# Inputs laid out by features, split without normalization, and 1/rms multiplied in after the products

## The chip, the cores and the metric

The kernel runs on one core of a Trainium2 chip. The metric is device time in microseconds (us) of one execution, as the median of several runs. The core has a matrix engine (TensorE; PE in the profile, PEld for its weight loads), three engines for elementwise work (VectorE is DVE, ScalarE is ACT, GpSimd is POOL), and SyncE (SP), which issues the DMAs in this kernel. Products land in PSUM, eight banks of 128 partitions x 512 float32.

## What is computed

Two transformer blocks, one after the other, on x of 256 tokens x 1024 features, in float32. Only the beginning of the first and the two memories matter here:

```python
h = rms_norm(x, g_pre_mix)                     # x / rms(x) * gain, over the 1024 features
q, k, v, z, xbc, dt_raw, ga, gs = split(h @ w_in)
o_att = stick_breaking_attention(q, k, v)      # 16 heads
o_ssm = ssm_branch(z, conv(xbc), dt_raw, ...)  # 32 heads, causal convolution of 4 taps, chunks of 128
merged = sigmoid(ga) * (o_att @ w_br_att) + sigmoid(gs) * (o_ssm @ w_br_ssm)
x = x + rms_norm(merged @ w_mix_out, g_post_mix)
x = x + rms_norm(memory_cross_attention(rms_norm(x, g_pre_xa), rms_norm(mem, g_mem), ...), g_post_xa)
x = x + rms_norm(swiglu(rms_norm(x, g_pre_ffn), ...), g_post_ffn)
# second block: two layers of attention (the first with a forget gate, "fox", the second with latent
# projections, "mla"), each also attending to rmsnorm(mem_2, mem_norm_2), and a convolved FFN
```

## The kernel before

The 256 tokens are two tiles of 128. Weights come from HBM in units of 128 x 1024 words (512 KB), and each is split into a high and a low float32r part, whose sum is the float32 value; activations are split in the same way. A product of two split values is three matmuls (high x high, high x low, low x high) that add up in one PSUM bank. The split of a unit is a copy to the high part (ACT, sometimes DVE) and a subtraction for the low part (DVE, sometimes POOL). Ten split units are held (NB) and four raw ones (RAW); SP's queue loads the next unit when a raw place is free.

All work is written as Python generators ("threads": main(0), main(1) for the tiles, mix_both, sb, ssd, memory, prepare for the weights and so on). Program.run() lets the thread go on that could start first by a rough model of the engines' times (class Model), with priorities, and so writes down the order of the instructions on each engine; that order is fixed in the program. A thread can wait for an event ("w"), a buffer of the arena ("b", "m"; 17,600 words for each partition in all), a bank ("p"), a split unit ("u") or a time ("r", "f"). A product is emitted only when its banks and its unit are there.

For a product the contraction must lie on the partitions, so the activations are needed transposed. prenorm_joint() (line 733) does this for x (g_pre_mix), mem (g_mem) and mem_2 (mem_norm_2): rms() squares the tile on ACT and sums it, rsqrt() adds and takes the power on POOL, two copies multiply the tile by 1/rms, transpose_split() (687) transposes its eight blocks on TensorE, and split_half() (701) multiplies by the gain and splits, block by block. The tiles' splits lie side by side in a Joint.

At the start build() (1960) loads x's first tile, the gains, two weight units, x's second tile and more units; first_consts() (1990) has TensorE run 22 transposes of the identity (WARM). main(t) (908) then makes its split and two products for v, which main(1) can make only after main(0) has begun the same unit. mix_both() (988) makes the products of both tiles at once that are wanted with the features on the partitions, by proj_joint() (768; two banks each): q and k (qk_both, 1025), dt (dt_both, 1085), B and C, and four groups of x and z. The convolved ones go through taps() (1038), which reads the bank for one ACT operation and three DVE operations for each of its two blocks; z goes through Silu (z_both, 1078). sb() does the stick-breaking attention in four lanes, ssd_quad() (1242) the state space model. In ssd_quad a row of acsT is spread over all partitions by a matmul with a column of pick (1254), both on 64 partitions, followed by matmuls that add a mask. memory() (1474) runs beside the rest: mem when the third of the four groups of the state space model is done, mem_2 after the first FFN's up products.

Nearly all elementwise operations are recorded at line 290, DMAs at 547, matmuls at 539 and transposes at 543, so in the profile they are told apart by tile names and shapes: wr is a raw unit, wh and wl its split, arena_r the split activations, pa PSUM, arena nearly everything else.

## Time and profile before

| | us |
|---|---|
| time, median of 3 runs (1333.91 to 1334.86) | 1334.74 |
| span of the profiled execution, from its first to its last instruction | 1330.6 |
| TensorE busy | 1289.8 |
| VectorE busy | 909.7 |
| ScalarE busy | 816.8 |
| GpSimd busy | 285.1 |

The times of the runs are of other executions than the profiled one, whose own time the profile gives only as its span. The profile's parts are: busy time by engine, the same in slices over the span, DMA queues, the chain of work that ended last, groups of instructions with mean duration and the idle time ahead of them, and the DMA issues. Matmuls are pipelined, so the duration of one is longer than the distance from its start to the next one's; where TensorE's pace is wanted, the distance between starts is read. A timeline row with "x2" holds two instructions that follow each other.

### The profile page before, as it was taken

What the parts mean: (1) busy time and instruction counts of PE and PEld (TensorE: products, weight loads), DVE (VectorE), ACT (ScalarE), POOL (GpSimd) and SP (SyncE); (2) the same over time, 40 slices, a digit from 0 to 9 for tenths busy, and PEclk for the clock granted to TensorE, in tenths of its full rate; (3) what the DMA queues carried; (4) which work ended last, traced back from release to release, by engine and by line L of the source; (5) the groups of instructions that cost most, each with busy time, mean ns of one, the idle gap of its engine ahead of it and who ended that gap; (6) DMA issues with size and microseconds to landing.
All of it is one profiled execution on the core that took longest, in us unless ns stands there. A gap on an engine that the chain in (4) does not pass through costs nothing.

```text
span 1330.6 us, 22067 instructions
## 1 busy us (share of the span) xinstructions
PE 1289.8 (97%) x8376; PEld 1146.3 (86%) x8376; DVE 909.7 (68%) x1471; ACT 816.8 (61%) x1481; POOL 285.1 (21%) x364
## 2 busy tenths in 40 slices
PE   8999999999999999999998899998999989999998
PEld 6989998898888887999997788788999867799997
DVE  6567688877677537655556567898665897786664
ACT  6567677766646547544456566785554785865552
POOL 3052203333022002000014521102111463031110
PEclk9999999999999999999999999998999999999999
DMA  8632543544664624756552343566654333365650
GB/s 270 219 112 96 195 154 107 180 158 143 216 211 159 227 73 143 246 183 188 190 192 96 127 143 112 191 221 221 190 185 144 115 112 99 131 223 189 185 173 32
DMA packets 62457, 217.95 MB, mean 164 GB/s; under 512 B 7440, under 2 KB 7568, under 8 KB 62352
## 3 DMA queue, kind: packets, MB, share of 16 engines
q1 hardware_dynamic: 62352, 216.56, 49.9%
q8 instruction: 65, 1.06, 0.3%
q14 instruction: 40, 0.33, 0.1%
HBM read 215.48 MB, written 1.05 MB: 163 GB/s over the span
## 4 chain that ended last, share of the span: by engine, by line
PE 79%; DVE 9%; POOL 5%; ACT 3%; issue 2%; DMA 2%; SPq 0%; DVEq 0%; POOLq 0%; ACTq 0%
PE pa L539 75%; DVE arena L290 6%; POOL arena L290 4%; PE pa L543 3%; DVE wl L290 2%; ACT arena L290 2%; POOL small L290 1%; ACT wh L290 1%; DVE arena_r L290 1%; DMA wr<-in_w_in 1%; ACT arena_r L290 0%; DMA arena<-in_mem 0%; DMA wr<-in_w_up 0%; DMA wr<-in_w_dn 0%; SPq L547 0%
## 5 line engine op out<-in xcount | busy, mean ns | idle before, releaser
L539 PE MATMUL pa<-wh,arena_r 128*128 128x512 f32 (+2 forms) x1812 | 590.8, 395 | 3.6 <-DVE arena_r L290 1.6
L290 DVE TENSOR_TENSOR wl<-wr,wh 128x1024 fp32r<-128x1024 f32 (+2 forms) x353 | 432.4, 1233 | 219.9 <-ACT wh L290 214.4
L290 ACT ACTIVATE wh<-wr 128x1024 fp32r<-128x1024 f32 (+3 forms) x393 | 406.2, 1044 | 246.5 <-PE pa L539 200.2
L539 PE MATMUL pa<-arena_r,wh 128*128 128x256 f32 (+2 forms) x2736 | 495.5, 283 | 0.0
L539 PEld LDWEIGHTS pa<-arena_r,wh 128*128 128x128 f32 (+2 forms) x2736 | 425.6, 190 | 4.3 <-issue 0.3
L539 PEld LDWEIGHTS pa<-wh,arena_r 128*128 128x128 f32 x1812 | 342.3, 190 | 73.2 <-DVE arena_r L290 3.3
L539 PE MATMUL pa<-arena_r,wl 128*128 128x256 f32 (+2 forms) x1368 | 385.5, 282 | 0.0
L539 PE MATMUL pa<-wl,arena_r 128*128 128x512 f32 (+2 forms) x906 | 353.2, 390 | 4.2 <-DVE wl L290 4.1
L539 PEld LDWEIGHTS pa<-arena_r,wl 128*128 128x128 f32 (+2 forms) x1368 | 259.9, 190 | 0.2
L290 POOL TENSOR_TENSOR wl<-wr,wh 128x1024 fp32r<-128x1024 f32 (+2 forms) x53 | 131.0, 2476 | 568.0 <-ACT wh L290 543.7
L539 PEld LDWEIGHTS pa<-wl,arena_r 128*128 128x128 f32 x906 | 172.0, 190 | 35.4 <-DVE wl L290 5.4
L290 ACT ACTIVATE arena<-pa 128x512 f32<-128x512 f32 (+4 forms) x142 | 78.5, 563 | 73.8 <-PE pa L539 58.9
L290 DVE SCALAR_TENSOR_TENSOR arena<-pa,cols,arena 128x255 f32<-128x255 f32 (+2 forms) x208 | 89.1, 476 | 31.2 <-ACT arena L290 29.6
L290 DVE TENSOR_TENSOR arena<-arena 128x512 f32<-128x512 f32 (+4 forms) x117 | 90.8, 792 | 23.1 <-POOL arena L290 13.3
L290 ACT ACTIVATE arena<-arena 128x512 f32<-128x512 f32 (+5 forms) x126 | 76.6, 615 | 33.7 <-DVE arena L290 30.6
L539 PE MATMUL pa<-arena 128*64 128x128 f32 (+4 forms) x888 | 91.2, 286 | 3.2 <-POOL arena L290 1.7
L539 PEld LDWEIGHTS pa<-arena 128*64 128x64 f32 (+3 forms) x888 | 78.1, 160 | 16.4 <-issue 5.5
L543 PE MATMUL pa<-ident,arena 128*128 128x128 f32 (+3 forms) x494 | 73.1, 278 | 18.1 <-DVE arena L290 14.0
L543 PEld LDWEIGHTS pa<-ident,arena 128*128 128x128 f32 (+3 forms) x494 | 56.8, 138 | 33.9 <-DVE arena L290 19.1
L290 POOL TENSOR_SCALAR small<-small 128x1 f32<-128x1 f32 x38 | 17.4, 459 | 265.6 <-ACT arena L290 186.9
L290 ACT ACTIVATE arena<-pa,cols 128x256 f32<-128x256 f32 x92 | 44.8, 566 | 28.2 <-PE pa L539 28.2
L290 ACT ACTIVATE arena<-pa,small 128x128 f32<-128x128 f32 (+4 forms) x126 | 44.5, 416 | 21.9 <-PE pa L539 21.6
(123 smaller groups left out, 769.8 us busy)
## 6 DMA issues: line engine op xcount, KB each, us to landing
wr<-in_w_up SPq DMA_DIRECT2D x96, 512.0 KB, 4.0
wr<-in_w_in SPq DMA_DIRECT2D x80, 512.0 KB, 4.3
wr<-in_w_gu SPq DMA_DIRECT2D x44, 512.0 KB, 4.1
wr<-in_w_dn SPq DMA_DIRECT2D x44, 512.0 KB, 4.2
wr<-in_w_down SPq DMA_DIRECT2D x22, 512.0 KB, 4.0
wr<-in_w_fox SPq DMA_DIRECT2D x20, 512.0 KB, 3.3
wr<-in_w_br_ssm SPq DMA_DIRECT2D x16, 512.0 KB, 4.2
wr<-in_w_xkv SPq DMA_DIRECT2D x16, 512.0 KB, 4.1
```

Of the source, the lines that this page charges most:

```text
L290: emit = (lambda: f(*a, **k)) if f else (lambda: None)
L539: self.T.matmul(out, l, r, start=start, stop=stop, skip_group_check=True)
L543: self.T.transpose(out, in_, self.const["ident"][:k, :k])
```

## The change

The host also lays out x, mem and mem_2 by features (x_T, mem_T and mem_2_T: 128 partitions, 8 blocks of features, 256 tokens). split_T() makes the split of (input * gain) from these, without transposes and without 1/rms, for both tiles at once. inv_rms() finds 1/rms of the tokens from the input as it was laid out before, which is loaded as well. Products with the tokens on the partitions are multiplied by 1/rms in the copy out of PSUM (a value for each partition); those with the features on the partitions by a [128, 256] tile R that has 1/rms of the tokens along each row, in a DVE multiplication (scaled()). spread() makes R: the identity times 1/rms, then a product with ones. For q and k the multiplication takes the place of the copy; for z, and ahead of the convolutions, it is an operation of its own, whose result goes to SBUF, from where Silu and the taps go on. Beside this, pick and acsT are used on all 128 partitions, with zeros in the upper 64, ones is set earlier, and the first loads come in another order. Comments and docstrings are left out of the file, so its lines have other numbers. The diff without these, cut to its core:

```diff
+    def load_T(self, name, half):
+        s = slice(1024 * half, 1024 * half + 1024)
+        self.dma(self.st["T", name].ap[:, s], self.d[name + "_T"][:, s])
+
+    def split_T(self, name, gain, X):
+        src = self.st["T", name].ap.rearrange("p (k t c) -> p k t c", k=8, t=2)
+        H, L = X.both
+        for k in range(8):
+            g = self.c(C_GAIN + 8 * GAINS.index(gain) + k)
+            yield self.act(H[:, k], src[:, k], "Copy", scale=g)
+            yield self.V.scalar_tensor_tensor(L[:, k], src[:, k], g, H[:, k].bitcast(F32), op0=OP.mult, op1=OP.subtract)
+            self.set((("T", name), k))
+
+    def inv_rms(self, name, t, x=None, r=None):
+        x = x or (yield from self.load_x(name, t))
+        r = self.st["r", name, t] = self.col() if r is None else r
+        yield from self.rms(x.ap, r)
+        x.free()
+        self.set(("r", name, t))
+
+    def spread(self, name):
+        w = yield ("b", 256)
+        for t in range(2):
+            yield ("w", ("r", name, t))
+            yield self.V.tensor_scalar(w.ap[:, 128 * t:128 * t + 128], self.const["ident"], self.st["r", name, t], None,
+                                       op0=OP.mult)
...
+        self.mm(b[1][:, :256], self.const["ones"], w.ap, True, True, 0.43)
+        yield self.copy(w.ap, b[1][:, :256])
...
     def main(self, t):
-        yield ("w", "ident")
-        x = st["x0", t]
         J = ("X", "g_pre_mix")
-        X = yield from self.prenorm_joint(t, x.ap, "g_pre_mix")
-        self.set(("first", "second")[t])
-        x.free()
+        X = st[J].tile(t)
         st["v", t] = yield ("b", D)
         for i in range(2):
-            b = yield from self.proj(X, self.cb("w_in", 4 + i), 2, 512)
-            yield self.copy(st["v", t].ap[:, 512 * i:512 * i + 512], b[1])
+            b = yield from self.proj(X, self.cb("w_in", 4 + i), 2, 512, parts=("T", "x"))
+            yield ("w", ("r", "x", t))
+            yield self.copy(st["v", t].ap[:, 512 * i:512 * i + 512], b[1], scale=st["r", "x", t])
...
-            yield self.act(sg.ap[:, s], b[1], "Sigmoid")
+            yield self.act(sg.ap[:, s], b[1], "Sigmoid", scale=st["r", "x", t])
...
+    def first_split(self):
+        st = self.st
+        yield from self.split_T("x", "g_pre_mix", st["X", "g_pre_mix"])
+        self.set("second")
+        st["T", "x"].free()
+        self.st["R"] = yield from self.spread("x")
+        self.set("R")
+
+    def scaled(self, dst, b, rows=slice(0, 128), scale=None):
+        d, p = (a.rearrange("p (f n) -> p f n", f=2)[rows] for a in (dst, b[1]))
+        if scale is None:
+            return self.V.tensor_tensor(d, p, self.by_rows()[rows], op=OP.mult)
+        return self.V.scalar_tensor_tensor(d, p, scale, self.by_rows()[rows], op0=OP.mult, op1=OP.mult)
...
     def mix_both(self, J):
-        yield ("w", (J, 1))
+        yield ("w", (("T", "x"), 7))
...
     def qk_both(self, bs, q, c):
+        yield ("w", "R")
             if q:
-                yield self.copy(st["qT"].ap[:, s], bs[i][1], scale=0.125)
+                yield self.scaled(st["qT"].ap[:, s], bs[i], scale=0.125)
             else:
                 for k in range(2):
-                    r = slice(64 * k, 64 * k + 64)
-                    yield self.copy(st["kT%d" % k].ap[r, s], bs[i][1][r])
+                    yield self.scaled(st["kT%d" % k].ap[:, s], bs[i], slice(64 * k, 64 * k + 64))
...
-    def taps(self, b, u, base, n):
+    def taps(self, b, u, base, n, norm=False):
         yield ("f", b[1])
+        x = None
+        if norm:
+            yield ("m", [512], [])
+            x = yield ("b", 512)
+            yield self.scaled(x.ap, b)
+            self.fbank(b)
+        u, p = (a.rearrange("p (j c) -> p j c", j=2) for a in (u, x.ap if norm else b[1]))
...
     def z_both(self, bs, g):
         for i in range(2):
-            yield self.act(z.ap[:, 512 * i:512 * i + 512], bs[i][1], "Silu")
+            yield self.scaled(z.ap[:, 512 * i:512 * i + 512], bs[i])
             self.fbank(bs[i])
+        yield self.act(z.ap, z.ap, "Silu")
...
     def ssd_quad(self, g, q, ys):
-                self.mm(b[1][:, 256 * j:256 * j + 256], const["pick"][:64, h:h + 1].to_broadcast([64, 128]),
-                        const["acsT"][:64, :], j == 0, False, 0.109)
+                self.mm(b[1][:, 256 * j:256 * j + 256], const["pick"][:, h:h + 1].to_broadcast([128, 128]),
+                        const["acsT"], j == 0, False, 0.109)
...
     def memory_norm(self, name, gain):
-        evs = [self.spawn(self.memory_tile(t, name, gain), self.cur.prio, 1) for t in range(2)]
+        st = self.st
+        st["T", name] = yield ("b", 2 * D)
+        for h in range(2):
+            self.load_T(name, h)
+        evs = [self.spawn(self.inv_rms(name, t), self.cur.prio, 1) for t in range(2)]
+        yield ("m", [], [2 * D, 2 * D])
+        X = st["X", gain] = Joint(self.memr)
+        yield from self.split_T(name, gain, X)
+        st["T", name].free()
         for e in evs:
             yield ("w", e)
...
     def memory(self):
         X = yield from self.memory_norm("mem", "g_mem")
+        R = yield from self.spread("mem")
             for i in range(2):
-                yield self.copy(st["kTx"].ap[:, 1024 * c + 512 * i:1024 * c + 512 * i + 512], bs[i][1])
+                k = st["kTx"].ap[:, 1024 * c + 512 * i:1024 * c + 512 * i + 512]
+                yield self.V.tensor_tensor(k.rearrange("p (f n) -> p f n", f=2), bs[i][1].rearrange("p (f n) -> p f n", f=2),
+                                           R.ap[:, None, :].to_broadcast([128, 2, 256]), op=OP.mult)
...
     def build(self):
-        for t in range(2):
-            self.st["x0", t] = self.buf(D)
-        list(self.load_x("x", 0, self.st["x0", 0]))
+        self.st["T", "x"] = self.buf(2 * D)
+        x = [self.buf(D) for _ in range(2)]
         g = slice(C_GAIN, C_CONV)
+        self.load_T("x", 0)
         self.dma(self.const["cols"][:, g], self.d["cols"][:, g])
         if not self.plan:
             self.load(2)
-        list(self.load_x("x", 1, self.st["x0", 1]))
+        self.load_T("x", 1)
+        if not self.plan:
+            self.load(RAW)
+        for t in range(2):
+            list(self.load_x("x", t, x[t]))
```

## Rows read from the trace of the kernel before

**Rows 1.** The page, part 1: busy time of each engine, its share of the span, instructions.
```profile
PE 1289.8 (97%) x8376; PEld 1146.3 (86%) x8376; DVE 909.7 (68%) x1471; ACT 816.8 (61%) x1481; POOL 285.1 (21%) x364
```
**Rows 2.** Windows by stage, from several questions: stretch in us, its length, busy time of PE, PEld, DVE, ACT and POOL (instructions), then TensorE's granted clock as a share of full, the busy share of the DMA engines, GB/s.
```profile
0.00:22.00 22.00, 16.22 (x71) 13.04 (x72) 13.14 (x18) 14.60 (x29) 7.88 (x14) 0.92 0.78 264
...
12.10:15.30 3.20, 3.17 (x8) 2.50 (x9) 3.13 (x9) 3.20 (x8) 0.00 (x0) 0.51 0.86 300
...
22.00:300.00 278.00, 275.01 (x2075) 251.62 (x2074) 199.11 (x311) 191.55 (x351) 80.70 (x108) 1.00 0.48 157
300.00:1331.00 1031.00, 998.57 (x6232) 881.64 (x6231) 697.49 (x1143) 610.66 (x1103) 196.50 (x245) 0.99 0.50 163
...
1000.00:1200.00 200.00, 190.32 (x1221) 164.96 (x1220) 161.95 (x323) 136.35 (x296) 64.97 (x75) 1.00 0.44 139
...
220.00:240.00 20.00, 19.48 (x183) 18.45 (x182) 18.07 (x29) 13.46 (x21) 6.11 (x3) 1.00 0.65 218
```
**Rows 3.** Waits of TensorE over the whole span, the largest: us in total, times, longest.
```profile
PE pa L543 <- DVE arena L290: 14.0, 10, 2.6
```
**Rows 4.** Timeline of TensorE at the start: start, us, instruction, in brackets the idle time before and what ended it.
```profile
9.09 0.47 PE L539 MATMUL pa<-wh,arena_r 128*128 128x512 f32 x1 [1.01 <-DVE wh L290]
10.26 0.50 PE L539 MATMUL pa<-wl,arena_r 128*128 128x512 f32 x1 [0.70 <-DVE wl L290]
12.13 1.22 PE L539 MATMUL pa<-wh,arena_r 128*128 128x512 f32 x2 [1.36 <-DVE arena_r L290]
...
16.20 0.39 PE L539 MATMUL pa<-wl,arena_r 128*128 128x512 f32 x1
16.42 0.62 PE L539 MATMUL pa<-wh,arena_r 128*128 128x512 f32 x2
16.88 0.39 PE L539 MATMUL pa<-wl,arena_r 128*128 128x512 f32 x1
```
**Rows 5.** Windows, of the matmuls of line 539 alone: stretch, its length, busy time of PE and PEld (instructions), granted clock, DMA share, GB/s.
```profile
0.00:21.40 21.40, 9.57 (x31) 6.73 (x31) 0.92 0.79 268
```
**Rows 6.** The chain that ended last in 0 to 80 us, in order of time: start, us, what.
```profile
21.40 41.76 PE pa L539 x290
```
**Rows 7.** Timeline of all engines at the start: the split of the first units, and 1/rms of x's second tile.
```profile
8.25 0.69 DVE L290 CAST wh<-wr 128x1024 fp32r<-128x1024 f32 x1 [1.32 <-DMA wr<-in_w_in]
8.98 1.23 DVE L290 TENSOR_TENSOR wl<-wr,wh 128x1024 fp32r<-128x1024 f32 x1
...
9.50 1.06 ACT L290 ACTIVATE wh<-wr 128x1024 fp32r<-128x1024 f32 x1 [1.45 <-DMA wr<-in_w_in]
...
14.72 0.66 ACT L290 ACTIVATE arena<-arena 128x512 f32<-128x512 f32 x1
...
16.56 1.55 POOL L290 TENSOR_TENSOR small<-small,mhalf 128x1 f32<-128x1 f32 x1
```
**Rows 8.** Groups of instructions of one shape over the whole span: busy us, mean ns of one, then the idle time before them and what ended it.
```profile
L539 PE MATMUL pa<-arena_r,wh 128*128 128x256 f32 x2688 | 489.0, 284 | 0.0
...
L290 DVE TENSOR_TENSOR arena_r<-arena,arena_r 128x256 fp32r<-128x256 f32 x66 | 29.9, 484 | 6.5 <-ACT arena_r L290 6.5
...
L290 DVE TENSOR_TENSOR arena<-pa,arena 128x512 f32<-128x512 f32 x37 | 25.3, 687 | 12.5 <-PE pa L539 11.4 <-ACT arena L290 1.1
L290 ACT ACTIVATE arena_r<-arena 128x256 fp32r<-128x256 f32 x66 | 24.6, 409 | 28.1 <-DVE arena L290 27.1 <-PE pa L539 1.0
...
L539 PE MATMUL pa<-arena 128*128 128x256 f32 x64 | 15.3, 384 | 0.5 <-DVE arena L290 0.5
...
L539 PE MATMUL pa<-acsT,pick 64*128 64x256 f32 x32 | 8.0, 329 | 0.0
```
**Rows 9.** Timelines where the memories are transposed (mem at 309.76, mem_2 at 696.54 us).
```profile
309.76 0.66 PE L543 MATMUL pa<-ident,arena 128*128 128x128 f32 x4 [1.75 <-ACT arena L290]
...
696.54 1.91 PE L543 MATMUL pa<-ident,arena 128*128 128x128 f32 x16
```
**Rows 10.** Timelines of TensorE in a product for both tiles (50 us) and in the state space model (198 us).
```profile
50.00 0.40 PE L539 MATMUL pa<-arena_r,wh 128*128 128x256 f32 x2
...
50.36 0.40 PE L539 MATMUL pa<-arena_r,wh 128*128 128x256 f32 x2
...
198.35 0.28 PE L539 MATMUL pa<-arena_r,wl 128*128 128x256 f32 x1
198.56 0.50 PE L539 MATMUL pa<-acsT,pick 64*128 64x256 f32 x2
198.99 0.28 PE L539 MATMUL pa<-negmaskT,identb 128*128 128x256 bf16 x1
199.20 0.50 PE L539 MATMUL pa<-acsT,pick 64*128 64x256 f32 x2
199.64 0.28 PE L539 MATMUL pa<-negmaskT,identb 128*128 128x256 bf16 x1
```
**Rows 11.** Timeline around 698 us: a weight split on POOL and an addition on DVE.
```profile
697.88 2.39 POOL L290 TENSOR_TENSOR wl<-wr,wh 128x1024 fp32r<-128x1024 f32 x1 [0.37 <-ACT wh L290]
698.33 2.49 DVE L290 TENSOR_TENSOR arena<-arena 128x512 f32<-128x512 f32 x1
```
**Rows 12.** Timeline of one group of heads of the stick-breaking attention: its first operation out of PSUM and a split of its output.
```profile
63.19 0.69 DVE L290 TENSOR_SCALAR arena<-pa 128x512 f32<-128x512 f32 x1 [0.82 <-PE pa L539]
...
77.41 0.38 ACT L290 ACTIVATE arena_r<-pa 128x256 fp32r<-128x256 f32 x1 [0.62 <-PE pa L539]
```

More of the change, by code (lines that the diff above doesn't have):

```diff
@@ L603, in row_done, with proj @@
             e[0].free()
-    def proj(self, X, keys, kper, width, k0=0):
+    def proj(self, X, keys, kper, width, k0=0, parts=None):
         yield ("p", 1)
@@ L731, in prenorm @@
         return X, r, ev
+    def load_T(self, name, half):
[21 more added lines that the diff above has]
+                                       op0=OP.mult)
+        yield ("w", "ones")
+        yield ("r", w.ap, self.const["ones"])
+        yield ("p", 1)
+        b = self.bank()
+        self.mm(b[1][:, :256], self.const["ones"], w.ap, True, True, 0.43)
+        yield self.copy(w.ap, b[1][:, :256])
+        self.fbank(b)
+        return w
     def prenorm_joint(self, t, src, name):
@@ L1048, in taps @@
                                             op0=OP.mult, op1=OP.add)
-        self.fbank(b)
+        if norm:
+            x.free()
+        else:
+            self.fbank(b)
     def conv_both(self, bs, i0, dst, ev):
-        evs = [self.spawn(self.taps(bs[i], dst.ap[:, 512 * i:512 * i + 512], C_CONV + 20 * i0 + 10 * i, 4))
+        evs = [self.spawn(self.taps(bs[i], dst.ap[:, 512 * i:512 * i + 512], C_CONV + 20 * i0 + 10 * i, 4, True))
                for i in range(2)]
@@ L1460, in gated_both @@
             self.set(("h", "w_gu", c, t))
-    def memory_tile(self, t, name, gain):
-        x = yield from self.load_x(name, t)
-        yield from self.prenorm_joint(t, x.ap, gain)
-        x.free()
     def memory_norm(self, name, gain):
-        evs = [self.spawn(self.memory_tile(t, name, gain), self.cur.prio, 1) for t in range(2)]
+        st = self.st
[7 more added lines that the diff above has]
+        st["T", name].free()
         for e in evs:
             yield ("w", e)
-        return self.st["X", gain]
+        for t in range(2):
+            self.set((("X", gain), t))
+        return X
     def memory(self):
@@ L1489, in memory @@
             for n in range(2):
-                yield self.copy(st["vx", n].ap[:, 512 * c:512 * c + 512], bs[n][1])
+                yield self.copy(st["vx", n].ap[:, 512 * c:512 * c + 512], bs[n][1], scale=st["r", "mem", n])
                 self.fbank(bs[n])
@@ L1917, in constants2 @@
         yield from tri(c["negmaskT"], 1, OP.is_ge, 0.0, -1e30)
-        yield G.memset(c["ones"], 1.0)
+        yield G.memset(c["acsT"][64:].bitcast(F32), 0.0)
+        yield G.memset(c["pick"][64:].bitcast(F32), 0.0)
         yield V.tensor_copy(c["identb"], c["ident"])
@@ L1970, in build @@
             self.load(2)
-        list(self.load_x("x", 1, self.st["x0", 1]))
+        self.load_T("x", 1)
+        if not self.plan:
+            self.load(RAW)
+        for t in range(2):
+            list(self.load_x("x", t, x[t]))
+        self.st["X", "g_pre_mix"] = Joint(self.memr)
         self.st["halo"] = self.buf(96)
@@ L1976, in build @@
         self.spawn(self.first_consts(), 0)
+        self.spawn(self.first_split(), 0, -0.5)
+        for t in range(2):
+            self.spawn(self.inv_rms("x", t, x[t]), 0, 0.5)
+        self.set("begun")
         if not self.plan:
-            self.load(RAW)
             self.spawn(self.prepare(), 0, lambda: self.urgency(self.unit_at))
@@ L1993, in first_consts @@
         self.set("ident")
+        yield self.G.memset(c["ones"], 1.0)
+        self.set("ones")
         b = self.bank()
@@ L2091, in layout @@
     d["x"], d["mem"], d["mem_2"] = a["x"][0], a["mem"][0], a["mem_2"][0]
+    for k in ("x", "mem", "mem_2"):
+        d[k + "_T"] = np.ascontiguousarray(d[k].T.reshape(8, 128, S).transpose(1, 0, 2)).reshape(128, 8 * S)
     pick = lambda n: a[n[:-2]][int(n[-1])] if n[-2] == "." else a[n].reshape(1024)
```

22 lines of the change are left out of this document (16 added, 6 removed).

## The prediction

> **What bounds the kernel now.** I read the page's busy times first: TensorE is busy for 97% of the span, VectorE (DVE) for 68%, ScalarE (ACT) for 61% [rows 1]. So time can go only where TensorE gets less to do, or where it stands still. The windows by stage tell where it stands: in 0 to 22 us it is busy for 16.2 of 22, in 22 to 300 us (the mixer, most of what the change touches) for 275.0 of 278, and after 300 us it stands 32.4 of 1031 us [rows 2]. The waits of TensorE say on whom: 14.0 us on DVE ahead of transposes, and everything else is smaller [rows 3]. Nothing in the mixer stands long, so a gain there must be instructions that TensorE no longer runs or runs faster, and a loss must be a new wait. At the start the reader should look at the gaps in the list of matmuls [rows 4]: the weight products begin at 9.09 us, stop for the low half of the weights and then for 1.36 us for the split of x, and get dense only after 13 us. In 12.10 to 15.30 us the granted clock was 0.51 of full [rows 2], so the lower level of 1.2 GHz, after a stretch in which the engine mostly stood.
>
> All terms are set against the profiled span, 1330.6 us. The median of the runs is 4.1 us above it (1334.74); I take that distance as unchanged.
>
> **Part 1, the start.** Up to 21.4 us TensorE has run 31 weight products [rows 5]. In the dense stretch a low-half product starts at 16.20 and the next at 16.88 us, with two high-half ones between [rows 4]: 0.68 / 3 = 0.227 us each. 31 x 0.227 = 7.0 us of useful work, so 21.4 - 7.0 = 14.4 us go to the warm-up, the 16 transposes of x and waiting. From 21.4 us on the chain shows TensorE alone for 41.8 us [rows 6], so a microsecond saved earlier arrives there whole.
> After the change the first product needs the first unit's weights and k blocks 0 to 3 of x_T. The weights come last: their high half is cast at 8.25 us, when the transfer has landed, and their low half is ready at 8.98 + 1.23 = 10.2 us [rows 7]; as many bytes lie ahead of them as before, with one DMA issue fewer. A block of x_T costs an ACT copy of 128x256 (0.41 us) and a DVE subtraction (0.48 us, a two-input DVE operation of that size) [rows 8], so four blocks take about 2 us of either engine and are done by 8 us. From then on both tiles can use each unit: 12 x 0.227 = 2.7 us of products for a unit whose split costs 1.06 us on ACT and 1.23 us on DVE [rows 7], so no wait for weights should follow. TensorE is thus dense from 10.2 us. It has less to do before that (its transposes go), so the low clock may fall into useful work: a stretch as long as the one seen, 3.2 us at 0.51, costs 1.6 us. x itself (1 MB more traffic, behind the first four units) costs nothing: 1/rms is wanted only when the first bank is full, near 20 us, and squares, sum and power took from 14.72 to 18.1 us for the second tile before [rows 7]. SP's queue holds the four loads of x ahead of the fifth unit; about 3 us of transfers, with 11 us of products in hand. So the 14.4 us become 10.2 to 13.5 (low clock 1.6, and 1.7 because DVE is full between 8 and 15 us); I take 11.6. Term: **-2.8 us** (-4.2 to -0.9).
>
> **Part 2, the transposes of both memories.** 32 leave TensorE. Sixteen in a row took 1.91 us [rows 9], 0.12 each: 3.8 us. For mem, spread() adds one matmul of 128x256 in plain fp32; such ones last 0.38 us [rows 8]. Both places lie within busy TensorE stretches, so **-3.4 us** (-1.0, if waits take their place, to -5.2, if the 1.75 us wait at 309.76 goes too [rows 9]). The eight copies by 1/rms leave ACT and DVE, and 32 splits of 128 columns become 16 of 256. I count nothing for that.
>
> **Part 3, pick and acsT on 128 rows.** This small edit takes time from TensorE itself. 256-column products on 128 rows follow each other by 0.12 us (three in the 0.36 us from 50.00 to 50.36) [rows 10]. Around the 64-row pair of pick and acsT they don't: 198.35 to 198.56 for the product ahead (0.21), 198.56 to 198.99 for the two (0.43), 198.99 to 199.20 for the mask (0.21), 199.20 to 199.64 for the next two (0.44) [rows 10]: 1.29 us for six instructions that take 0.72 at 0.12 each. The 32 of them [rows 8] make eight such groups: 8 x 0.57 = 4.6 us. They last 329 ns where 128 rows with as many columns last 284 [rows 8], so rows and not columns seem to be the reason; the mixer's TensorE is full [rows 2], so it counts. Term: **-4.6 us** (-4.6 to 0).
> The Trainium skill speaks on both sides. TensorE: Matmul & The Clock Gate, section LDWEIGHTS (loading the stationary operand), says that a weight load's time goes by columns and not by the rows of the contraction; by that this term would be 0 and the sum 1331.5. TensorEngine Tiling (Array Packing), section Key Properties, says that a change of tiling mode drains the engine, and has 64 rows as a mode; by that the gaps are drains, and the sum stays. The rows show gaps around every 64-row pair, so the trace is with the second.
>
> **Part 4, work added beside TensorE in the mixer.** DVE must now do what either engine did, or nobody: q and k, 12 operations (4 + 8); z, 8; the banks ahead of the convolutions, 12; the memory's keys, 4. A DVE operation of 128x512 with a PSUM source takes 0.69 us [rows 8]: 36 x 0.69 = 25 us, some of it on DVE before; I count 23 new. ACT gives up the copies of k and part of q and z. The taps of the convolutions read SBUF instead of PSUM; that costs where GpSimd (POOL) works beside them: an addition of 128x512 within SBUF took 2.49 us under a POOL split of 2.39 us [rows 11]. In the mixer DVE had 199 us of 278, and 18.07 of 20 in a full window [rows 2]; with 23 more it has 222, or 80%. In 1000 to 1200 us it is 81% busy and TensorE stands 9.7 us of 200 (waits of the attention are in that too), while in the mixer it stands 3.0 of 278 [rows 2]. At that rate the mixer would stand 13.5 us, 10.5 more. The bounds are 0 and +10.5. A bank comes free after one operation now where a convolution held it through all taps, and POOL, idle for 70% there, can take weight splits; so I take **+3 us**, nearer to the rows of this stage than to those of attention.
>
> **Sum:** -2.8 - 3.4 - 4.6 + 3 = -7.8; 1330.6 - 7.8 = 1322.8 us of span, 1326.9 measured. A planner places all instructions by times that move with every edit, so the later stages may come in another order, and the 32 us that TensorE stands there could shift by an estimated 3 us (a tenth) either way. I put no sign on it.
>
> **Rivals.**
> *The added DVE work eats the gain.* For it: the full windows [rows 2] and the slowdown beside POOL [rows 11]. Against it: ACT and POOL have room. 1326.9 - 3 + 10.5 = 1334.4, no change.
> *Pick saves nothing,* as the columns alone would have it: 1326.9 + 4.6 = 1331.5.
> *The start gets no denser,* by the low clock or the longer queue of transfers: 1326.9 + 2.8 = 1329.7.
> *Slower: room in the arena.* Its 17,600 words hold kT0, kT1 and qT (6,144), v (2,048), B and C (2,048), xT and zT of two groups (4,096) and their xdt (2,048) when the stick-breaking attention runs beside the products: 16,480 with the halo. Of the 1,120 left, R now keeps 256 to the mixer's end, and each convolution bank wants 512 before it can be given back; so does each attention lane, which holds its 512 from 63.19 to about 77.4 us [rows 12]. Where they collide, two of the eight banks stay held for part of these 14 us. If B, C and the first two groups of x each stop TensorE for a quarter of that, 4 x 3.5 = 14 us are lost: 1326.9 + 14 = 1341 us. It decides once banks are held for longer than the products in reach can cover; the planner runs other products meanwhile, which speaks against it.
>
> **Chances.** Forecast 0.54, start without gain 0.04, pick without gain 0.08 (half of it on either side of the bound), gain eaten 0.20, arena 0.14. The measurement can tell 0.2%, or 2.7 us, from no change, so faster means under 1332.1 and slower over 1337.4. Faster: 0.54 + 0.04 + 0.04 = 0.62; same: 0.04 + 0.20 = 0.24; slower: 0.14. The forecast alone spans about 1321 to 1332 (its terms at their bounds, with the mixer at 0 to +6, not all at once). The range takes in the eaten case with its spread and leaves out most of the arena: 1320 to 1338.
>
> **What would show it.** Start: products dense from about 10.2 us, and about 43 of them by 21.4 us instead of 31. Pick: 0.12 us from each to the next. Memories and x: 48 transposes fewer. Mixer: TensorE's idle time in 22 to 300 us; 6 us is my forecast, over 13 the eaten case, and long holes with DVE and ACT idle the arena. I am wrong if the later stages move by more than 3 us, which no row here can show.

## The result, and the profile of the changed kernel

The changed kernel takes 1346.33 us (median of four runs, 1344.36 to 1347.96), the kernel before 1334.77 in the same rounds: 1.0093 times as long, interval 1.0076 to 1.0111, or 11.6 us slower. The forecast was 1326.9 us. The profiled execution took 1347.96 us, with a span of 1346.2.

The page's busy times of the changed kernel, to be laid beside [rows 1]:

```profile
PE 1288.8 (96%) x8332; PEld 1149.1 (85%) x8332; DVE 932.9 (69%) x1474; ACT 802.5 (60%) x1430; POOL 309.3 (23%) x378
```

TensorE has 44 instructions fewer and is busy for 1.0 us less, although its span is 15.6 us longer. DVE is busy for 23.2 us more. That this is the 23 I had counted is chance: DVE runs 12 weight splits of 128x1024 fewer (328 in 402.6 us instead of 340 in 422.0), and its 72 convolution taps are busy for 42.6 us instead of 33.6, because some of them were held up, as will be seen. ACT has lost 14.3, and POOL has gained 24.2, which I had not counted. The windows by stage, with the columns of [rows 2], show where the time went:

```profile
0.00:22.00 22.00, 16.56 (x65) 13.62 (x66) 11.02 (x17) 14.01 (x24) 5.89 (x18) 0.84 0.80 300
22.00:300.00 278.00, 265.51 (x2050) 247.85 (x2049) 215.31 (x324) 179.63 (x318) 92.55 (x89) 0.99 0.47 156
...
300.00:700.00 400.00, 389.77 (x2344) 345.99 (x2343) 243.03 (x312) 210.41 (x321) 58.47 (x74) 0.99 0.54 178
```

In 22 to 300 us TensorE stands for 12.5 us, where it stood for 3.0 [rows 2]. So the loss is in the mixer, the stage that the change edits. SP's timeline dates it: each line is the first load of the weights w_mix_out, which comes as the mixer ends, of the kernel before and of the changed one.

```profile
362.42 0.33 SPq L547 DMA_DIRECT2D wr<-in_w_mix_out  x1
```
```profile
374.91 0.33 SPq L547 DMA_DIRECT2D wr<-in_w_mix_out  x1
```

There the changed kernel is 12.5 us behind. The same distance read at the first load of w_br_att is 2.3 us ahead (60.08 against 62.39), at that of w_br_ssm 3.8 behind (174.83 against 170.98), and at that of w_up, two stages further on, 12.6 behind (814.27 against 801.66). The start gained, the loss comes between 60 and 375 us, and the stages behind it keep the distance (11.0 at the first load of w_q_up, 1044.28 against 1033.26; 15.6 at the end of the span, in the longest of the four executions). TensorE's waits name several engines where [rows 3] had one large item, DVE's arena writes; the next two of the kernel before, POOL's arena writes and DVE's wl, were 4.1 us each:

```profile
PE pa L543 <- DVE arena L290: 10.1, 7, 2.6
PE pa L539 <- DVE wl L290: 9.4, 3, 5.5
PE pa L543 <- ACT arena L290: 8.6, 3, 5.6
PE pa L539 <- ACT arena L290: 7.6, 5, 3.1
```

One of these stops, traced back. The timeline of all engines of the changed kernel around 160 us, ahead of the first chunk products of the state space model (of the matmuls, only the one that waited):

```profile
158.25 2.40 POOL L290 TENSOR_TENSOR wl<-wr,wh 128x1024 fp32r<-128x1024 f32 x1 [2.45 <-DMA wr<-in_w_in]
...
158.70 9.10 DVE L290 SCALAR_TENSOR_TENSOR arena<-arena,cols 128x255 f32<-128x255 f32 x12 [0.18 <-ACT arena L290]
...
161.17 2.56 POOL L290 TENSOR_TENSOR wl<-wr,wh 128x1024 fp32r<-128x1024 f32 x1 [0.51 <-ACT wh L290]
...
167.89 1.06 ACT L290 ACTIVATE arena<-arena 128x1024 f32<-128x1024 f32 x1 [4.55 <-DVE arena L290]
...
169.00 1.65 PE L539 MATMUL pa<-arena 128*128 128x128 f32 x6 [2.65 <-ACT arena L290]
```

Read from below: TensorE stood for 2.65 us for ACT's Silu, which had waited 4.55 us for the twelve convolution taps on DVE, which took 9.10 us. Twelve at 0.477, the mean in the kernel before (its group is shown with e6), are 5.7. A timeline of DVE alone, cut to 158.6 to 160.5 us, shows one tap by itself:

```profile
158.70 2.24 DVE L290 SCALAR_TENSOR_TENSOR arena<-arena,cols 128x255 f32<-128x255 f32 x1 [0.18 <-ACT arena L290]
```

It began while POOL's weight split ran (158.25 to 160.65) and lasted until 160.94. The split that starts at 161.17 holds another tap in the same way. What follows the stop is read from windows (columns as above) laid on three stretches, each of which begins at the end of a stop or shortly before it:

```profile
168.40:171.90 3.50, 2.90 (x13) 2.90 (x14) 1.75 (x3) 2.44 (x3) 0.98 (x1) 0.51 0.43 150
243.50:247.00 3.50, 3.39 (x17) 3.39 (x17) 3.06 (x7) 2.83 (x12) 0.93 (x2) 0.51 0.03 11
315.20:322.00 6.80, 4.66 (x11) 3.74 (x12) 6.49 (x14) 3.38 (x7) 3.51 (x4) 0.50 0.53 193
```

In these stretches, 13.8 us together, TensorE's clock is at the lower of its levels, 1.2 GHz. Not every stop brings one: TensorE also stood for 2.79 us ahead of 268.99, and in 264 to 275 us the granted clock was 1.00. The kernel before had a granted clock of 1.00 over 22 to 300 us [rows 2].

The stop of 5.5 us on DVE's wl at 317 us has another origin. The timeline of POOL, DVE and TensorE there:

```profile
300.89 11.32 POOL L290 TENSOR_SCALAR arena<-arena 128x1 f32<-128x1 f32 x32
...
312.25 0.18 DVE L290 TENSOR_SCALAR arena<-arena 128x32 f32<-128x32 f32 x1 [6.27 <-POOL arena L290]
...
313.56 2.34 POOL L290 TENSOR_TENSOR wl<-wr,wh 128x1024 fp32r<-128x1024 f32 x1
313.62 2.53 DVE L290 TENSOR_SCALAR arena<-arena 128x32 f32<-128x32 f32 x2
316.06 1.22 DVE L290 TENSOR_TENSOR wl<-wr,wh 128x1024 fp32r<-128x1024 f32 x1
...
317.34 0.80 PE L539 MATMUL pa<-wl,arena_r 128*128 128x512 f32 x1 [5.49 <-DVE wl L290]
```

These are angles() (the cosines for the second block): 32 small POOL operations, and DVE stood for 6.27 us at the head of its queue until they were done, with the weight split that TensorE needed behind. Then a POOL split held two tiny DVE operations for 2.53 us. The kernel before has this work too; DVE stood for 4.25 us there (at 302.41).

### The profile page after: what moved, and what is told of

It reads as the page before. It is cut to its first block, busy times and chain, and to the rows that moved or that the text cites. A ratio compares the mean times of both kernels' runs of the same rounds, so it can differ in the third digit from the quotient of the medians.

```text
span 1346.2 us, 21976 instructions
## 1 busy us (share of the span) xinstructions
PE 1288.8 (96%) x8332; PEld 1149.1 (85%) x8332; DVE 932.9 (69%) x1474; ACT 802.5 (60%) x1430; POOL 309.3 (23%) x378
## 4 chain that ended last, share of the span: by engine, by line
PE 75%; DVE 12%; POOL 4%; ACT 4%; issue 3%; DMA 2%; SPq 0%; POOLq 0%; DVEq 0%; ACTq 0%
PE pa L539 72%; DVE arena L290 8%; POOL arena L290 3%; PE pa L543 3%; ACT arena L290 2%; DVE wl L290 2%; DVE arena_r L290 1%; ACT wh L290 1%; DMA wr<-in_w_in 1%; POOL small L290 1%; ACT arena_r L290 0%; DMA wr<-in_w_up 0%; POOL wl L290 0%; DMA wr<-in_w_dn 0%; DMA wr<-in_w_br_ssm 0%
## 5 line engine op out<-in xcount | busy, mean ns | idle before, releaser
L290 ACT ACTIVATE wh<-wr 128x1024 fp32r<-128x1024 f32 (+2 forms) x395 | 407.4, 1043 | 264.4 <-PE pa L539 216.6
L290 DVE TENSOR_TENSOR wl<-wr,wh 128x1024 fp32r<-128x1024 f32 (+2 forms) x341 | 413.0, 1219 | 213.1 <-ACT wh L290 209.1
L290 POOL TENSOR_TENSOR wl<-wr,wh 128x1024 fp32r<-128x1024 f32 (+2 forms) x65 | 159.4, 2461 | 586.6 <-ACT wh L290 517.2
L290 ACT ACTIVATE arena<-arena 128x512 f32<-128x512 f32 (+5 forms) x130 | 80.6, 626 | 58.4 <-DVE arena L290 56.5
L543 PE MATMUL pa<-ident,arena 128*128 128x128 f32 (+3 forms) x446 | 65.9, 279 | 19.8 <-DVE arena L290 10.1
L290 ACT ACTIVATE arena<-pa 128x512 f32<-128x512 f32 (+3 forms) x96 | 52.4, 555 | 50.0 <-PE pa L539 33.1
L290 DVE SCALAR_TENSOR_TENSOR arena<-arena,cols 128x128 f32<-128x128 f32 (+3 forms) x152 | 77.0, 535 | 6.7 <-ACT arena L290 5.3
L543 PEld LDWEIGHTS pa<-ident,arena 128*128 128x128 f32 (+3 forms) x446 | 51.8, 138 | 34.2 <-DVE arena L290 12.2
L290 DVE SCALAR_TENSOR_TENSOR arena<-pa,cols,arena 128x255 f32<-128x255 f32 (+1 forms) x136 | 57.7, 477 | 23.9 <-ACT arena L290 22.6
L290 ACT ACTIVATE arena<-pa,small 128x128 f32<-128x128 f32 (+3 forms) x142 | 54.1, 443 | 30.9 <-PE pa L539 30.6
```

The costliest lines, as they stand in the source:

```text
L290: emit = (lambda: f(*a, **k)) if f else (lambda: None)
L543: self.T.transpose(out, in_, self.const["ident"][:k, :k])
```

## The experiments

Four theories stood against each other. **Blocked taps:** the convolution now reads a buffer in SBUF instead of the bank, and DVE operations on two SBUF operands wait out a POOL weight split. **DVE's load:** it is the 23 us of added work. **Arena:** the new buffers hold others up. **Order:** the planner's new order is worse, whatever the work. Ratios are to the kernel before, run on the same chip.

**e1, pick alone.** The kernel before with pick and acsT on 128 rows, zeros in the upper 64. The order is held: TensorE's queue is the same to the instruction, and on ACT and DVE one part of a weight split each stands one or two places earlier.

```diff
-self.mm(..., const["pick"][:64, h:h + 1].to_broadcast([64, 128]), const["acsT"][:64, :], ...)
+self.mm(..., const["pick"][:, h:h + 1].to_broadcast([128, 128]), const["acsT"], ...)
```

> The kernel before, with only pick and acsT widened to 128 rows (zeros below). If the 64-row matmuls cost TensorE its drains, the 0.57 us of each of the eight groups go and the time is 1334.8 - 4.6 = 1330.2 us (1329 to 1331.5). If rows do not matter, 1334.8. If any edit that moves the planner's times is worth several us by the new order alone, the time may lie anywhere within some 5 us of 1334.8, with the distance of the six instructions of a group still at 0.7 us instead of 1.3.

Measured: 1329.92 us, 0.9968 (0.9955 to 0.9981), 4.3 us less by the ratio (3.6 between the medians of the same rounds). In the changed kernel's timeline the group of [rows 10] looks like this:

```profile
236.61 0.39 PE L539 MATMUL pa<-acsT,pick 128*128 128x256 f32 x2
236.85 0.28 PE L539 MATMUL pa<-negmaskT,identb 128*128 128x256 bf16 x1
236.89 0.48 PE L539 MATMUL pa<-acsT,pick 128*128 128x256 f32 x2
237.21 0.28 PE L539 MATMUL pa<-negmaskT,identb 128*128 128x256 bf16 x1
```

The product ahead begins at 236.50 in the same list, so the six instructions take 0.71 us (236.50 to 237.21) where they took 1.29; in e1's own timeline they take 0.72 (234.70 to 235.42). The term is confirmed by itself.

**e2, e3, e4: three single edits of the changed kernel.** e2 multiplies by 1/rms in place in the bank, so that the taps read PSUM as before and no buffer is taken. e3 lets angles() wait for the first FFN's up products. e4 calls the taps without norm: it leaves out 1/rms ahead of the convolutions, with its multiplication and its buffer.

```diff
 # e2, in taps()
-            yield ("m", [512], [])
-            x = yield ("b", 512)
-            yield self.scaled(x.ap, b)
-            self.fbank(b)
+            yield self.scaled(b[1], b)      # the bank is given back at the end
 # e3, in angles()
-        yield ("w", ("o", 1, 2))
+        yield ("w", ("w_gu", "up"))
 # e4, in conv_both()
-... C_CONV + 20 * i0 + 10 * i, 4, True)
+... C_CONV + 20 * i0 + 10 * i, 4)
```

> The changed kernel, but the banks ahead of the convolutions are multiplied by 1/rms in place, in PSUM, and the taps read the bank as in the kernel before. The number of DVE operations stays. Theory A (taps out of SBUF, slowed beside POOL, and 512 more words of arena): the taps go back from 0.76 to 0.48 us where POOL works, the stops of TensorE at 166 and 266 us go, and the time falls by 4 to 8 us to 1338 to 1342. Rival B (the stop at 311 us behind the 32 small POOL operations of the angles): the time stays within 2 us of 1346. Rival C (order alone): any time within 5 us.

> The changed kernel, but the thread of the angles waits for the first FFN's up products instead of the third group of the state space model. Theory B: the stop of 5.65 us at 311 us and the low clock behind it (about 3 us) go, 1346.3 - 8 = 1338 us. Theory A: the stop only moves to the next late split of a weight, and the time stays within 3 us of 1346.

> The changed kernel with the multiplication by 1/rms ahead of the convolutions left out (B, C and the x of the state space model stay unnormalized): 12 DVE operations of 0.69 us fewer, no extra buffers, the taps read PSUM. Theory A: as in the run that scales in PSUM, and up to 3 us less, 1336 to 1341. Theory B: within 2 us of 1346. If DVE's load as such were the cause, this gains more than scaling in PSUM does, by about as much as the 8.3 us of DVE weigh.

Measured: e2 1335.08 us, 1.0005 (0.9990 to 1.0021); e3 1341.76, 1.0053 (1.0030 to 1.0077); e4 1329.73, 0.9977 (0.9955 to 0.9998). e2 has the same multiplications on DVE as the changed kernel (12 of them, now into PSUM) and wins back 11 us, which speaks against the added work itself as the loss. The twelve taps at the place shown above, in e2:

```profile
158.08 5.15 DVE L290 SCALAR_TENSOR_TENSOR arena<-pa,cols,arena 128x255 f32<-128x255 f32 x12 [0.37 <-ACT arena L290]
159.97 2.41 POOL L290 TENSOR_TENSOR wl<-wr,wh 128x1024 fp32r<-128x1024 f32 x1 [1.67 <-ACT wh L290]
...
166.13 0.94 PE L539 MATMUL pa<-arena 128*128 128x128 f32 x6 [0.52 <-ACT arena L290]
```

Here too a POOL split runs beside them, and they take 5.15 us instead of 9.10; TensorE stands for 0.52 us instead of 2.65. e4 removes one DVE operation for each bank beside that and gains another 5 us, part of it by not doing the work. e3 is 4.6 us faster than the changed kernel, where 8 were expected if the hold by angles() were the cause. e2 and e4 came out 3 and 6 us under their ranges. None of these three keeps the order, so their sizes are not clean.

**e5 to e8.** e5 is e2 with the 512-word buffer taken and held though unused, and the bank held too. e6 is the changed kernel with taps from SBUF, and no weight splits on POOL until the mixer ends. e7 is e2 with 39 warm-up transposes in place of 22. e8 is e2 with both memories normalized and transposed on TensorE as before.

```diff
 # e6 (the same key in the stages start, sb, ssd and mixed; ssd had 0.4, the others the default 0.8)
+TUNE = {'mixed': dict(POOL=50.0), ...
 # e7
-WARM = 22
+WARM = 39
```

> As the run that scales in PSUM, but each bank's taps also take the 512 words of arena that the changed kernel takes, and hold them unused (the bank is held as well). If room in the arena is what costs (the fourth rival of the prediction), the gain of scaling in PSUM goes and the time is again near 1346 us. If the SBUF source of the taps is what costs, it stays within 2 us of the run that scales in PSUM, 1335.

> The changed kernel, but the planner puts no weight split on POOL up to the end of the mixer; DVE does them all. If taps that read two SBUF operands are held up by a POOL split that runs beside them (2.0 to 2.6 us instead of 0.48), all taps take 0.48 us again and the stop at 166 us goes, while DVE has some 25 x 1.23 = 31 us more to do: between 1338 and 1348 us, by which of the two is dearer. If DVE's load is the cause and not the contention, it is clearly slower than 1346, 1352 and more. With theory C no statement.

> As the run that scales in PSUM, with 39 transposes of the identity at the start instead of 22, so that TensorE works until the first weight product at 9 us. If the low clock at the start takes back the gain of the earlier products, the granted clock stays full there, the products run at 0.227 us from the first one, and the time falls by 1.7 to 3.4 us to 1332 to 1333. If the start is not on the path, it stays at 1335.

> As the run that scales in PSUM, with both memories normalized, transposed and split as in the kernel before. By the prediction's second part it is 3.4 us slower, 1338.5. If the copies and splits of the memories are what counts and not the transposes, or if the late multiplication of the keys costs as much, 1335 or less.

Measured: e5 1340.44 us, 1.0050 (1.0032 to 1.0068); e6 1329.48, 0.9964 (0.9950 to 0.9978); e7 1333.36, 1.0000 (0.9989 to 1.0012); e8 1337.66, 1.0027 (1.0013 to 1.0042).

e6 is the opposite of e2: the SBUF operands stay and POOL's splits go, DVE has 8.5 us more to do in 22 to 300 us, and 17 us are gained, 9 more than the better end of what was expected. The groups of instructions of one shape in 22 to 330 us, columns as in [rows 8], first the changed kernel, then the kernel before, e2 and e6:

```profile
L290 POOL TENSOR_TENSOR wl<-wr,wh 128x1024 fp32r<-128x1024 f32 x28 | 69.8, 2509 | 134.4 <-ACT wh L290 94.4 <-PE pa L539 36.8 <-DMA wr<-in_w_in 2.5
...
L290 DVE SCALAR_TENSOR_TENSOR arena<-arena,cols 128x255 f32<-128x255 f32 x24 | 18.4, 771 | 0.9 <-ACT arena L290 0.8
L290 DVE SCALAR_TENSOR_TENSOR arena<-arena,cols 128x254 f32<-128x254 f32 x24 | 13.2, 568 | 0.4
...
L290 DVE SCALAR_TENSOR_TENSOR arena_r<-arena,cols,arena_r 128x256 fp32r<-128x256 f32 x4 | 7.5, 1884 | 0.0
```
```profile
L290 POOL TENSOR_TENSOR wl<-wr,wh 128x1024 fp32r<-128x1024 f32 x18 | 46.5, 2586 | 148.5 <-ACT wh L290 148.5
...
L290 DVE SCALAR_TENSOR_TENSOR arena<-pa,cols,arena 128x255 f32<-128x255 f32 x24 | 11.5, 477 | 5.7 <-ACT arena L290 5.7
```
```profile
L290 POOL TENSOR_TENSOR wl<-wr,wh 128x1024 fp32r<-128x1024 f32 x27 | 69.5, 2586 | 138.2 <-ACT wh L290 82.3 <-PE pa L539 55.2 <-issue 0.7
...
L290 DVE SCALAR_TENSOR_TENSOR arena<-pa,cols,arena 128x255 f32<-128x255 f32 x24 | 11.3, 476 | 1.8 <-ACT arena L290 1.8
...
L290 DVE SCALAR_TENSOR_TENSOR arena_r<-arena,cols,arena_r 128x256 fp32r<-128x256 f32 x8 | 8.7, 1092 | 0.0
```
```profile
L291 DVE SCALAR_TENSOR_TENSOR arena<-arena,cols 128x255 f32<-128x255 f32 x24 | 11.5, 480 | 0.5 <-ACT arena L291 0.5
...
L291 DVE SCALAR_TENSOR_TENSOR arena_r<-arena,cols,arena_r 128x256 fp32r<-128x256 f32 x8 | 3.8, 481 | 1.2 <-ACT arena_r L291 1.1
```

Both conditions are needed. Taps from PSUM take 0.476 to 0.477 us with 18 or 27 POOL splits in the stretch; taps from SBUF take 0.480 without POOL splits and 0.771 on average with 28. The last line of the e2 group shows it within one kernel: another DVE operation, with its operands still in SBUF, takes 1.092 us there, 0.481 in e6. The Trainium skill has the rule (SBUF — State Buffer, section Who interferes with whom): a DVE instruction with two SBUF inputs needs the read port that it shares with GpSimd, and the one that comes second waits for the whole of the other, it isn't slowed in proportion. The tap of 2.24 us under a split of 2.40 agrees.

e5 was to be near 1335 or near 1346 and is at neither. It has no new stops in the mixer (268.75 us busy in 22 to 300, e2 268.78), is level with e2 at the first load of w_q_up (1031.5 against 1031.8) and loses its time behind it, where the edited taps don't run, so it speaks against the arena theory there, and for order as a cost of its own. e7 and e8 price two terms of the sum, below.

**e9 to e12: the order.** e9 is the kernel before without POOL splits in the mixer (e6's edit). e10 and e11 are the kernels before and after with the planner's latency between engines at 0.18 us instead of 0.17: the same work, placed anew by the planner, which sets the order and, where an operation has two forms, the engine. e12 puts e6, 39 warm-ups and e3 together.

```diff
-    LAT = 0.17
+    LAT = 0.18
```

> The kernel before, with no weight split on POOL up to the end of the mixer. If the splits on POOL hurt the changed kernel because its taps read two SBUF operands, the kernel before, whose taps read PSUM, gains little: 1331 to 1337 against 1334. If POOL splits in the mixer are bad for any kernel of this kind, it gains as the changed one did (17 us): below 1325.

> The kernel before, its planner's latency between engines 0.18 instead of 0.17 us: the same instructions in a slightly other order. This measures theory C, what an order is worth by itself. If order alone explains the 11.6 us, it moves by 5 us and more; if not, by less than 3 us.

> The changed kernel with the same planner's latency of 0.18 us. By theory A (POOL splits beside taps out of SBUF) the loss is of the work and stays: 1340 to 1350, with taps of over 2 us beside POOL splits. By theory C it may come anywhere, down to 1335 too.

> The changed kernel without POOL splits in the mixer, with 39 transposes of warm-up and the angles later: what the runs so far point to. If the three gains add up, 1329.5 - 1.7 - 4.6 = 1323; if the stop at 302 us that is left without POOL splits is not the angles', 1328.

Measured: e9 1344.79 us, 1.0092 (1.0067 to 1.0118); e10 1345.41, 1.0095 (1.0071 to 1.0120); e11 1354.80, 1.0169 (1.0137 to 1.0201); e12 1334.86, 1.0011 (0.9997 to 1.0025). This was the surprise of the study: 0.01 us in a model parameter costs the kernel before as much as the whole change did. e11 lies 5 us above its range. e9, expected at 1331 to 1337, lost 12 us by its new order; of the two kernels planned without POOL's splits in the mixer, the changed one (e6) is 15 us faster than the kernel before (e9). And e12, made of three edits that each had helped, is 5 us slower than e6 alone. So differences between two kernels that the planner ordered anew hold a share of order of several us, e2 to e6 among them, and an experiment at a held order was needed.

**e13 and e14: held order.** The planner runs as it did and each instruction keeps its place in the order, but where it had put a weight split of the mixer on POOL, DVE runs it. e13 is this on the changed kernel, e14, the control, on the kernel before. TensorE's and ACT's queues are the same to the instruction.

```diff
         o[1].bias = self.cfg["POOL"]
+        if self.cfg.get("HOLD"):         # set in the stages start, sb, ssd and mixed
+            o[1].emit = o[0].emit
```

> The changed kernel with every instruction in its place, as planned, except that the weight splits which the planner gave to POOL up to the end of the mixer are emitted on DVE at the same point of the program; TensorE's and ScalarE's queues are the same to the instruction. If taps (and other DVE operations on two SBUF operands) that wait out a POOL split are what costs, the long taps go and the time falls by 4 us or more, 1336 to 1342. If the loss is the order, it stays at 1344 to 1348 or rises with DVE's load.

> The control: the kernel before in its own order, with its mixer's POOL splits emitted on DVE. Its taps read PSUM, so by theory A it gains little or nothing: 1331 to 1338. If it gains as much as the changed kernel does, the gain is not the taps'.

Measured: e13 1334.41 us, 1.0021 (1.0005 to 1.0037); e14 1333.97, 1.0011 (0.9988 to 1.0034). The control gains nothing, the changed kernel gains 0.72%, 9.6 us, more than the 4 us that were asked of it. That POOL is a slow place for a weight split can't be the reason: in the changed kernel's trace none of TensorE's waits is for a low half written by POOL. In e13's groups the taps are at their plain duration, and its mixer ends 10.3 us sooner:

```profile
L291 DVE SCALAR_TENSOR_TENSOR arena<-arena,cols 128x255 f32<-128x255 f32 x24 | 11.4, 478 | 0.1
```
```profile
364.63 1.69 SPq L550 DMA_DIRECT2D wr<-in_w_mix_out  x2
```

The edit frees more than the taps. In 22 to 375 us the 72 taps are busy for 9.0 us less than in the changed kernel (33.6 instead of 42.6), but DVE's 36 additions within SBUF also fall from 29.1 to 23.5 us, and its 6 copies of units to the high part from 6.4 to 4.0. The kernel before has held additions too (28.8 us, 23.3 in e14) and gained nothing when they were freed, and e2, in which the taps alone are out of POOL's way, has most of the gain; so the taps are the likely main part, but no run at a held order has them alone.

**e15 to e18: two more orders.** Both kernels at a latency of 0.16 and of 0.175 us.

> The kernel before with the planner's latency at 0.16 us: one more order of the same work. If its usual order is a lucky one, again 1340 to 1350; if 0.18 was an unlucky one, 1331 to 1338.

> The changed kernel with the planner's latency at 0.16 us. If the change's work costs 5 us or more in any order, it is that much slower than the kernel before at the same latency; if order is all, either may be the faster one.

> The kernel before with the planner's latency at 0.175 us. If its usual order is a lucky one, 1338 to 1350; otherwise near 1334.

> The changed kernel with the planner's latency at 0.175 us. If the change's work costs something in any order, it is slower than the kernel before at the same latency, by 5 us or more; if order is all, either may be faster.

Measured, with the pairs from above:

| planner's latency | before | after | after less before |
|---|---|---|---|
| 0.16 (e15, e16) | 1344.94 | 1358.58 | 13.6 |
| 0.17 (as given) | 1334.77 | 1346.33 | 11.6 |
| 0.175 (e17, e18) | 1343.71 | 1351.76 | 8.1 |
| 0.18 (e10, e11) | 1345.41 | 1354.80 | 9.4 |

By the ratios to the kernel before of the same rounds, the order given to the kernel before is 10 to 13 us better than its neighbours, that of the changed kernel 5 to 13. The difference between the two is 8 to 14 us in each of four orders, so the loss belongs to the change and not to bad luck with its order. The held taps are there in all four: those of 255 columns take 0.63 to 0.77 us on average in the changed kernels, with 23 to 28 POOL splits in 22 to 330 us, and 0.477 in the kernels before, with 17 to 21.

## Why the prediction was wrong

**Part 1, the start: right, a little large.** I said -2.8 us, the first load of w_br_att comes 2.3 sooner (1.5 to 2.6 in the four orders). 40 weight products were begun by 21.4 us (31 before, 43 foreseen). TensorE's timeline at the start:

```profile
9.13 0.79 PE L539 MATMUL pa<-wh,arena_r 128*128 128x512 f32 x1 [3.56 <-ACT wh L290]
10.39 0.79 PE L539 MATMUL pa<-wl,arena_r 128*128 128x512 f32 x1 [0.47 <-DVE wl L290]
10.98 1.05 PE L539 MATMUL pa<-wh,arena_r 128*128 128x512 f32 x2
...
15.30 0.40 PE L539 MATMUL pa<-wl,arena_r 128*128 128x512 f32 x1
```

The products are dense from 10.98 us (10.2 foreseen), but a window on 8.02 to 14.85 us shows a granted clock of 0.50: TensorE stood for 3.56 us for the first weights, where it had transposed x before, and the clock was at 1.2 GHz for 6.8 us, twice the 3.2 that I had carried over. That is this execution; e2, whose start is nearly the same, has a granted clock of 0.92 over 0 to 22 us where this one has 0.84. In e7 the longer warm-up leaves no such stretch (granted clock 1.00 in 0 to 22 us, 46 products by 21.4), and the kernel is 0.7 us (by the ratios) to 1.7 us (by the medians) faster than e2, which the intervals don't separate.

**Part 2, the memories: in agreement, not proven.** -3.4 us foreseen; e8 against e2 gives 2.6 by the medians, 2.9 by the ratios. But both were planned anew, and a new order alone was worth 10 us and more.

**Part 3, pick: right, and for its reason.** -4.6 foreseen, -4.3 measured at a held order. By what the Trainium skill (TensorE: Matmul & The Clock Gate, section LDWEIGHTS (loading the stationary operand)) says, that columns and not rows decide, it would have been 0. The gaps went with the 64 rows, which agrees with the drains that the Trainium skill (TensorEngine Tiling (Array Packing), section Key Properties) names; that they are drains no run shows.

**Part 4, the work beside TensorE: the step that failed.** I priced it by how long TensorE stands where DVE is as busy (+3, at most +10.5); by the account below it cost 21 us. The row with the mechanism was there: an addition of 2.49 us under a POOL split of 2.39 [rows 11]. I named it, for the taps, and then let it vanish in an average, as a few more microseconds of DVE time. The right question was what one tap that waits out a whole split holds up: the Silu, and behind it the state space model's products, for which TensorE stood. I also counted POOL's room for more splits as help. It took 28 in 22 to 330 us in place of 18, and each was a chance to block a tap. And I counted stops alone, when three of the five longest in the mixer brought a stretch at half the clock.

The mixer's account, from windows of 22 to 375 us: the first group is e13, the second its control e14 (300 to 375 us: the last quarter).

```profile
22.00:375.00 353.00, 342.46 (x2485) 314.03 (x2484) 277.01 (x437) 228.25 (x383) 49.44 (x103) 0.99 0.50 166
...
300.00:375.00 75.00, 72.38 (x409) 62.41 (x409) 52.19 (x77) 42.22 (x56) 7.26 (x25) 0.95 0.58 193
```
```profile
22.00:375.00 353.00, 348.42 (x2515) 315.80 (x2515) 258.05 (x422) 238.20 (x423) 47.94 (x104) 1.00 0.49 163
...
300.00:375.00 75.00, 73.67 (x450) 64.64 (x449) 53.45 (x97) 48.85 (x79) 5.16 (x20) 1.00 0.55 184
```

At the end of the mixer the changed kernel should have been ahead by the start (2.3), pick (3.9 at this mark in e1) and mem (2.3, e8 against e2): 8.5 us. It was 12.5 behind, so the mixer lost 21. With the blocking by POOL's splits taken away (e13) it is 2.2 behind: the blocking is 10.3 of the 21. These are marks of single executions, good to a few us: the same distance between the changed kernel and e13 is 14.8 at the first load of w_up and 12.5 at that of w_q_up, and 9.6 by the ratios. (TensorE's standing in 22 to 375 us: 19.6 us in the changed kernel, 10.5 in e13, 4.7 in the kernel before.) The other 10.7 are still there in e13: TensorE stands 6.0 us more than in the control, and the lower clock, 0.97 in 235 to 300 us and 0.95 in 300 to 375 against 1.00 in the control, makes an estimated 5.7 (0.03 x 65 + 0.05 x 75, from clocks rounded to a hundredth). The two longest stops of e13 there, which the control doesn't have (its longest is 1.74 us):

```profile
241.37 0.27 PE L542 MATMUL pa<-negmaskT,identb 128*128 128x256 bf16 x1 [3.00 <-ACT arena L291]
...
308.20 0.79 PE L542 MATMUL pa<-wl,arena_r 128*128 128x512 f32 x1 [2.62 <-DVE wl L291]
```

The second lies behind angles(), for which DVE stood 5.57 us (at 305.25). Ahead of the first ACT waited for an addition on DVE, which had worked almost without a pause since 227.5 us; shortly before the addition stands a weight split of 1.22 us that the edit had moved there from POOL. In the changed kernel this stop is as long, 3.13 us at 243.61, but by the other cause: four splits of activations took 3.11 us beside POOL, 1.13 in e13. So e13 trades one for the other here, and the 10.3 may be too small. How much of the rest is the added work and how much the order stays open; the sum of stops and clock, 11.7, is near my upper bound of 10.5, which was the rival in which the added work eats the gain.

**The order: wrong by a factor of three and more.** I allowed ±3 us for it, in the later stages. The kernel before moves by 10 to 13 us when it is only planned anew. This isn't what sank the forecast: the later stages of the changed kernel kept the distance of 12.5 us to within about 3.

**The rivals.** Pick without gain and a start without gain are refuted by e1 and by the load's date. The arena rival gave nearly the right time (1341) for a reason that no run bears out: e5, with the buffer held, has e2's stops in the mixer; its price in later stages isn't settled. The true case, DVE against POOL in SBUF, was no rival of its own; it stood as a remark in the first one, which put it at no change.

The best versions are e6 at 1329.48 us, the change without POOL's splits in the mixer, and e1 at 1329.92, the edit of pick alone; the two can't be told apart, and both beat both kernels. Not tried: the planner's parameters tuned anew for the change, and the taps' source alone at a held order.

## What to carry to other kernels

Before a two-operand DVE operation moves from PSUM to SBUF, look up what POOL runs beside it: where POOL works on SBUF, allow for the operation waiting out the whole of POOL's instruction, and follow who waits for it, instead of adding to a busy share. Where a planner writes the order, measure first how far the kernel moves when a parameter changes by a trifle, and test a cause with the order held, with a control. A stop of TensorE costs more than its length when the clock falls behind it.

## What the runs showed of the hardware that was not expected

A DVE tap with two SBUF operands that began 0.45 us after a POOL split ended 0.29 us after it, and so took 2.24 us instead of 0.48. DVE operations with one SBUF input can be held too: two of 128x32, 0.39 us in the kernel before (at 308.53), took 2.53 beside another split, and copies of a unit to the high part 1.074 on average in the changed kernel, 0.702 in e13. In the kernel before, moving POOL's splits of the mixer to DVE made DVE only 5.2 us busier in 22 to 375 us (258.05 us against 252.89), although it ran 17 weight splits more there, 20.9 us at 1.227 each: its own splits, 1.299 us on average with POOL's beside them, fell to 1.227, and its additions of 128x512 within SBUF from 0.841 to 0.686.
